# Turning attention probabilities with VectorE blocks and DMA through DRAM, in a one-core two-layer kernel

## The chip, the core and the metric

The kernel runs on one core of a Trainium2 chip. The metric is device time in microseconds of one launch; smaller is better. Before the change the median of three runs is 840.81 us (840.78 to 840.98).

## The reference

The model has two layers on a sequence of 512 tokens of width 1024, everything in float32: first a state-space layer, then a multi-head latent attention layer with 16 heads. The change touches only the second layer. Cut to what it computes there:

```python
def causal_block_attention(q, k, v, scale):          # 16 heads, 512 queries and keys
    s = jnp.einsum('bqhd,bkhd->bhqk', qb, k).astype(jnp.float32) * scale
    s = jnp.where(key_pos[None, :] <= q_pos[:, None], s, -jnp.inf)
    p = jax.nn.softmax(s, axis=-1)
    return jnp.einsum('bhqk,bkhd->bqhd', p, v)

def mla_mixer(u, positions, in_w, q_norm_w, kv_norm_w, uq_w, ukv_w, out_w):
    c_q, c_kv, k_r, z = split(u @ in_w)
    q = rms_norm(c_q, q_norm_w) @ uq_w               # per head 128 + 64 with rotary position
    kv = rms_norm(c_kv, kv_norm_w) @ ukv_w           # per head 128 of k, 128 of v
    o = causal_block_attention(q_full, k_full, v, 192 ** -0.5)
    return (o.reshape(bsz, seq, 2048) * jax.nn.silu(z)) @ out_w

h = h + y                                            # after each layer
return rms_norm(h, final_norm_w)
```

Softmax is taken over the keys of one query, so it is natural to hold scores with the query on the partition. The product with `v` sums over keys, so it wants the key on the partition. The probabilities therefore have to be turned between the two. The residual `h` is turned as well, once: the layers hold it with the feature on the partition, the last step (final norm and output) with the token on the partition.

## The kernel before, in words

**Precision.** A matmul in full precision is done as three matmuls on numbers split into a high part (`hi`, type float32r) and a low part (`lo`, the rest): hi·hi, hi·lo, lo·hi. ScalarE (ACT) makes `hi` with a cast, VectorE (DVE) makes `lo` with a subtraction. This holds for the weights (`split_weight`, tiles `whi`, `wlo`), for activations (`ah`, `al`, `vh`, `vl`, `ch`, `cl`, `qh`, `ql`, `k`) and for the turned probabilities (`ph`, `pl`).

**Weights.** They are streamed: `weight` asks for a tile of a fixed list, and `prefetch` keeps one tile split and one further tile loading ahead. There are two buffers for raw tiles and three for the split ones. All loads are issued by SyncE (SP), which takes its instructions strictly in order and stands still at one whose wait is not met.

**Order of work.** The order on TensorE (PE) is that of the program text. The order on the other engines is made by a scheduler when the program is built; it is fixed then, and each engine takes its instructions in that order. `sched(feed, pieces)` weaves small pieces into a long stream of projections (the feed): a piece is put behind the first projection chunk at which the cost that has gone by reaches the number in a table.

**The attention layer** (`mla`). After six first projections (`U_M1`, loop over `i`) and norms, the heads are worked in pairs: `front_a(j)` projects the rotary part, q and k of the even head, `front_b(j)` q and k of the odd head and v of both, `zgemm` one tile of the gate z. For head `h` the feed is one of the fronts for a later pair, then a `zgemm`, and from head 11 on chunks of the output projection. Into this feed three kinds of pieces are woven, each with its table of shares of the feed's cost:

- `score(h + 1, b)`, table `SC` = 0.0, 0.16, 0.25, 0.44: for the query block `b` of the next head, five matmuls into PSUM (three for block 0), then on DVE the mask and row minimum (L804, L806), on ACT the exponential with its row sum (L223), on DVE the reciprocal (L808) and the scaling (L809). Result: `p`, 128 queries x n keys, n = 128, 256, 384, 512.
- `turn(h, kb)`, table `TU` = 0.02, 0.08, 0.38, 0.55: TensorE transposes (L818) the blocks of key block `kb` of this head, 4, 3, 2 and 1 of 128x128 each, into PSUM tile `pt`; ACT casts them to `ph` (L822), DVE subtracts to `pl` (L823).
- `product(h, kb)`, table `PR` = 0.3, 0.48, 0.65, 0.94: three matmuls (L836) with v; after the last, DVE multiplies with the gate (L838).

In the profile of before, the segment of one head is the stretch from the L797 of `score(h + 1, 0)` to the next L797. "Even" segments are those in which an even head is turned and multiplied; `front_a` runs in them, and so do its four small DMAs `rsw` (L697) that swap 32-partition pieces for the rotary embedding.

**The residual.** In the loop over the six first projections, at i = 2 to 5, TensorE transposes `h` (L682, 32 transposes of 128x128), ACT copies (L685) and SP stores to the DRAM tensor `hd` (L686). It is loaded again much later for the output (L924).

## Time and profile before

| | |
|---|---|
| median of 3 runs | 840.81 us |
| the profiled execution's own time | 840.15 us |
| its span, first to last instruction | 838.3 us |
| granted TensorE clock, mean | 0.998 |
| attention heads, from the first transpose of probabilities to the last | 507.8 to 777.2 us |
| two heads (from one group of `rsw` DMAs at 545.2 to the next at 580.4, 614.9, 650.1) | some 35 us |

The page says for each engine how long it was busy, then shows the span in 40 slices, the DMA queues, and the chain of work that ended last. The trace behind it can be asked for single instructions: start, duration, operation, output and input tiles, and the idle time before with what ended it. A matmul of 512 columns is shown with some 0.39 us, but the next one starts 0.23 us later, since they are pipelined; so the cost of a matmul on TensorE is the distance between starts, not its duration.

### The profile page before, as it was taken

The page shows a single profiled execution, that of the slowest core. Times are in us where ns is not written, and L with a number is a line of the kernel's source. Part 1 is how long each engine was busy: PE and PEld are TensorE (multiplying, and loading weights), DVE is VectorE, ACT ScalarE, POOL GpSimd, SP SyncE. Part 2 cuts the span into 40 slices and gives each one's busy share as a digit, 9 for nine tenths or more (in the row PEclk, how much of TensorE's full clock was granted, in tenths as well). Part 3 has the DMA queues.
Part 4 walks back from the last instruction along what each step waited for, and adds up shares of the span by engine and source line. Part 5 has one row for each costly group of instructions (what it writes and reads, how often), then busy time and mean ns, then how long its engine had stood idle before and what let it go on. Part 6 is the DMA issues. An engine that isn't in the chain of part 4 may idle for free.

```text
span 838.3 us, 11586 instructions
## 1 busy us (share of the span) xinstructions
PE 822.8 (98%) x4260; PEld 694.8 (83%) x4260; DVE 640.2 (76%) x1226; ACT 453.5 (54%) x802; POOL 0.2 (0%) x4
## 2 busy tenths in 40 slices
PE   7999999999999999999999999999999999999996
PEld 5887888888888888888888888888888888888885
DVE  7899898979788979776564887786767869675544
ACT  7567755545565657333354664456547557554233
POOL 0000000000000000000000000000000000000000
PEclk9999999999999999999999999999999999999999
DMA  6354543434242424323225242222221224331212
GB/s 227 102 186 145 153 150 106 147 101 128 98 151 76 151 87 137 121 95 101 90 86 176 79 129 64 77 65 73 73 64 56 89 75 157 100 100 53 92 59 100
DMA packets 35112, 90.55 MB, mean 108 GB/s; under 512 B 4784, under 2 KB 6320, under 8 KB 35056
## 3 DMA queue, kind: packets, MB, share of 16 engines
q1 hardware_dynamic: 34336, 88.77, 32.9%
q10 hardware_dynamic: 720, 1.05, 0.3%
q8 instruction: 33, 0.54, 0.3%
q14 instruction: 23, 0.19, 0.1%
HBM read 83.12 MB, written 4.33 MB: 104 GB/s over the span
## 4 chain that ended last, share of the span: by engine, by line
PE 91%; DVE 5%; DMA 2%; ACT 1%; issue 1%; SPq 0%; DVEq 0%; ACTq 0%
PE mm L291 54%; PE ot L942 11%; PE s L794 5%; PE mm L300 4%; PE po L836 4%; PE mm L774 3%; PE pt L818 2%; PE yd L138 2%; PE yd L291 1%; PE aux L130 1%; PE aux L105 1%; DMA x<-in_x_dram 1%; PE aux L77 1%; PE aux L89 1%; DMA L<-ac_d 1%; DVE wlo L273 1%
## 5 line engine op out<-in xcount | busy, mean ns | idle before, releaser
L272 ACT CAST whi<-raw 128x1024 fp32r<-128x1024 f32 (+3 forms) x132 | 127.0, 965 | 214.7 <-PE mm L291 177.4
L273 DVE TENSOR_TENSOR wlo<-raw,whi 128x1024 fp32r<-128x1024 f32 (+3 forms) x132 | 146.8, 1115 | 56.1 <-ACT whi L272 55.8
L291 PE MATMUL mm<-ah,whi 128*128 128x512 f32 x384 | 153.9, 401 | 0.0
L291 PE MATMUL mm<-ah,wlo 128*128 128x512 f32 x384 | 150.1, 391 | 0.4 <-DVE wlo L273 0.4
L291 PE MATMUL mm<-al,whi 128*128 128x512 f32 x384 | 149.8, 390 | 0.0
L291 PE MATMUL mm<-vh,whi 128*128 128x512 f32 x224 | 89.6, 400 | 0.9 <-ACT whi L272 0.9
L291 PE MATMUL mm<-vh,wlo 128*128 128x512 f32 x224 | 87.8, 392 | 0.7 <-DVE wlo L273 0.7
L291 PE MATMUL mm<-vl,whi 128*128 128x512 f32 x224 | 87.5, 391 | 0.0
L291 PEld LDWEIGHTS mm<-ah,wlo 128*128 128x128 f32 x384 | 72.1, 188 | 16.0 <-DVE wlo L273 0.8
L291 PEld LDWEIGHTS mm<-ah,whi 128*128 128x128 f32 x384 | 72.2, 188 | 15.5 <-issue 1.4
L291 PEld LDWEIGHTS mm<-al,whi 128*128 128x128 f32 x384 | 72.2, 188 | 14.4 <-DVE al L312 0.3
L942 PE MATMUL ot<-whi,ah 128*128 128x512 f32 (+1 forms) x136 | 52.3, 384 | 0.0
L942 PE MATMUL ot<-whi,al 128*128 128x512 f32 (+1 forms) x136 | 51.4, 378 | 0.0
L942 PE MATMUL ot<-wlo,ah 128*128 128x512 f32 (+1 forms) x136 | 51.4, 378 | 0.0
L291 PEld LDWEIGHTS mm<-vh,wlo 128*128 128x128 f32 x224 | 42.0, 188 | 10.8 <-DVE wlo L273 1.5
L291 PEld LDWEIGHTS mm<-vh,whi 128*128 128x128 f32 x224 | 42.1, 188 | 9.2 <-ACT whi L272 1.1
L223 ACT ACTIVATE p<-p,st 128x128 f32<-128x128 f32 (+1 forms) x64 | 36.1, 564 | 25.1 <-DVE st L806 25.0
L291 PEld LDWEIGHTS mm<-vl,whi 128*128 128x128 f32 x224 | 42.2, 188 | 7.2
L822 ACT CAST ph<-pt 128x512 fp32r<-128x512 f32 (+1 forms) x64 | 26.5, 422 | 33.2 <-PE pt L818 32.8
L291 PE MATMUL mm<-ch,whi 128*128 128x512 f32 x104 | 42.6, 409 | 0.0
L291 PE MATMUL mm<-ch,wlo 128*128 128x512 f32 x104 | 40.8, 392 | 0.0
L291 PE MATMUL mm<-cl,whi 128*128 128x512 f32 x104 | 40.7, 392 | 0.0
(225 smaller groups left out, 1642.6 us busy)
## 6 DMA issues: line engine op xcount, KB each, us to landing
raw<-in_w_dram SPq DMA_DIRECT2D x100, 512.0 KB, 3.3
L<-ac_d SPq DMA_DIRECT2D x32, 256.0 KB, 3.8
E<-ea_d SPq DMA_DIRECT2D x32, 128.0 KB, 3.3
raw<-in_ua_dram SPq DMA_DIRECT2D x8, 512.0 KB, 3.3
raw<-in_ub_dram SPq DMA_DIRECT2D x8, 320.0 KB, 2.9
x<-in_x_dram SPq DMA_DIRECT2D x8, 256.0 KB, 4.3
res<-in_x_dram SPq DMA_DIRECT2D x8, 256.0 KB, 3.3
hd<-ht SPq DMA_DIRECT2D x8, 256.0 KB, 2.3
```

What stands on the lines that cost most here:

```text
L138: nc.tensor.matmul(yd[64 * h:64 * h + 64, s], self.xdt[j][:, c, h, :], self.L[2 * j + h][:, s], start=True, stop=True)
L223: i = self.nc.scalar.activation(out, in_, func, **k)
L272: nc.scalar.copy(hi[:, a:b], raw[:, a:b])
L273: nc.vector.tensor_tensor(lo[:, a:b], raw[:, a:b], hi[:, a:b].bitcast(F32), op=ALU.subtract)
L291: self.nc.tensor.matmul(ps, a, b, start=i == 0, stop=i == len(seq) - 1)
L300: self.nc.tensor.matmul(p, seq[i][0], seq[i][1], start=i == 0, stop=i == 3 * ks - 1)
L774: nc.tensor.matmul(ps[:, c2 * 256:(c2 + 1) * 256], a, b, start=i == 0, stop=i == 5)
L794: nc.tensor.matmul(ps[:, :n], x[:, s], y[:, :n], start=k == 0, stop=k == 4)
L818: nc.tensor.transpose(pt[:, (b - kb) * P:(b - kb + 1) * P], probs[h][b][:, kb * P:(kb + 1) * P], self.ident)
L822: nc.scalar.copy(ph[:, :n], pt[:, :n])
L836: nc.tensor.matmul(po[:, kb * P:], x, y, start=kb == 0 and k == 0, stop=kb == NCH - 1 and k == 2)
L942: nc.tensor.matmul(ps[:, a:b], x, y, start=start and i == 0, stop=stop and i == 5)
```

## The change

It takes the transposes of the probabilities and of the residual off TensorE. VectorE's `transpose` turns each 32x32 block of a tile within itself; what is left is to put whole blocks in each other's places. That is done by four DMAs for a tile, one for each band of 32 partitions, that store to a DRAM tensor with runs of 32 numbers (128 bytes). For the probabilities these are two tensors `pd` of 512x512, one for even and one for odd heads; `turn` then loads the turned rows of a key block as `pl`, from which ACT casts `ph` and DVE subtracts in place. There are two buffers `pb` for the turned tiles and one `pl` for each key block. For the residual the same is done with eight tiles of 128x512, stored straight into `hd`.

Two tables change: `SF` puts the scores of head 0 into the feed one projection sooner (`front_b(0)` and `zgemm(4)` are now one feed), and `PR0` puts the products of head 0 later in their feed. The tiles that `norm` uses get other names, so that `pl` is not among them.

```diff
-SF = (0.02, 0.1, 2.1, 3.1)
+SF = (1.0, 1.4, 3.4, 5.0)
+PR0 = (0.5, 0.62, 0.75, 0.95)
...
         hd = self.dram.tile([NCH, P, D], F32, name="hd")
+        turned = hd[:].rearrange("c (j a) d -> a (c j) d", a=32)
...
             if i >= 2:
-                c = i - 2
-                for n in range(2):
-                    pt = self.bank("pt")
-                    for k in range(4):
-                        nc.tensor.transpose(pt[:, k * P:(k + 1) * P], self.h[4 * n + k][:, c * P:(c + 1) * P],
-                                            self.ident)
-                    ht = wk.tile([P, T], F32, tag=("ph", "pl")[n], name=self.nm("ht"))
-                    nc.scalar.copy(ht[:], pt[:])
-                    nc.sync.dma_start(hd[c, :, n * T:(n + 1) * T], ht[:])
+                for k in (2 * i - 4, 2 * i - 3):
+                    ht = wk.tile([P, T], F32, tag="ph", name=self.nm("ht"))
+                    v.transpose(ht[:], self.h[k][:])
+                    for b in range(4):
+                        m = slice(32 * b, 32 * b + 32)
+                        nc.sync.dma_start(turned[:, :, k * P + 32 * b:k * P + 32 * b + 32],
+                                          ht[m, :].rearrange("a (j b) -> a j b", b=32))
...
-        probs = [[] for _ in range(MH)]
+        pd = [self.dram.tile([T, T], F32, name=f"pd{i}") for i in range(2)]
...
             v.tensor_scalar(p[:], p[:], st[:, 2:3], None, op0=ALU.mult)
-            probs[h].append(p)
+            pb = wk.tile([P, T], F32, tag="pb", name=self.nm("pb"))
+            v.transpose(pb[:, :n], p[:])
+            turned = pd[h % 2][:].rearrange("(j a) q -> a j q", a=32)
+            for i in range(4):
+                q = b * P + 32 * i
+                nc.sync.dma_start(turned[:, :n // 32, q:q + 32],
+                                  pb[32 * i:32 * i + 32, :n].rearrange("a (j q) -> a j q", q=32))
...
         def turn(h, kb):
             n = T - kb * P
-            pt = self.bank("pt")
-            for b in range(kb, NCH):
-                nc.tensor.transpose(pt[:, (b - kb) * P:(b - kb + 1) * P], probs[h][b][:, kb * P:(kb + 1) * P],
-                                    self.ident)
+            pl = wk.tile([P, n], F32R, tag=f"pl{kb}", name=self.nm("pl"), bufs=1)
+            nc.sync.dma_start(pl[:].bitcast(F32), pd[h % 2][kb * P:(kb + 1) * P, kb * P:])
             ph = wk.tile([P, T], F32R, tag="ph", name=self.nm("ph"))
-            pl = wk.tile([P, T], F32R, tag="pl", name=self.nm("pl"))
-            nc.scalar.copy(ph[:, :n], pt[:, :n])
-            v.tensor_tensor(pl[:, :n], pt[:, :n], ph[:, :n].bitcast(F32), op=ALU.subtract)
+            nc.scalar.copy(ph[:, :n], pl[:].bitcast(F32))
+            v.tensor_tensor(pl[:], pl[:].bitcast(F32), ph[:, :n].bitcast(F32), op=ALU.subtract)
             parts[h].append((ph, pl))
...
-            at = (wk, ("qh", "ql", "s2") if n == KVL else ("ph", "pl", "s2"))
+            at = (wk, ("qh", "ql", "s2"))
...
-        self.run(front_b(0))
-        self.sched(zgemm(4), [(x, functools.partial(score, 0, b)) for b, x in enumerate(SF)])
+        self.sched(chain(front_b(0), zgemm(4)), [(x, functools.partial(score, 0, b)) for b, x in enumerate(SF)])
...
-            pieces += [(x * cost, functools.partial(product, h, b)) for b, x in enumerate(PR)]
+            pieces += [(x * cost, functools.partial(product, h, b)) for b, x in enumerate(PR0 if h == 0 else PR)]
```

**Where the instructions stand now, SyncE.** The place is the segment of an even head (head 6): its turned probabilities are `pd0`, those of the next, odd head are `pd1`. `raw` are weights, `rsw` the rotary swaps. Before, SP held only these for the two heads:

```order
L263 DMA raw_1149_5729<-in_ub_dram 128x640
L263 DMA raw_1181_5848<-in_uc_dram 128x512
L263 DMA raw_1192_5909<-in_w_dram 128x1024
L697 DMA rsw_1163_5775<-rraw_1162_5773 32x512 x4
L263 DMA raw_1215_5991<-in_ua_dram 128x1024
L263 DMA raw_1231_6057<-in_w_dram 128x1024
```

Now, from the odd head's block 0 on:

```order
L815 DMA pd1_4157<-pb_1152_5847 32x4x32 x4
L823 DMA pl_1153_5853<-pd0_4156 128x512
L823 DMA pl_1155_5858<-pd0_4156 128x384
L697 DMA rsw_1158_5868<-rraw_1157_5866 32x512 x4
L815 DMA pd1_4157<-pb_1165_5901 32x8x32 x4
L815 DMA pd1_4157<-pb_1169_5919 32x12x32 x4
L823 DMA pl_1175_5946<-pd0_4156 128x256
L264 DMA raw_1177_5951<-in_uc_dram 128x512
L815 DMA pd1_4157<-pb_1184_5976 32x16x32 x4
L823 DMA pl_1185_5991<-pd0_4156 128x128
L264 DMA raw_1188_6017<-in_w_dram 128x1024
L823 DMA pl_1196_6047<-pd1_4157 128x512
```

Every load of the even head's probabilities (`pl` from `pd0`) has come to stand behind stores of the next head's scores (`pd1`), which wait for VectorE.

**VectorE, the same segment.** Before, with `p` the scores of the odd head and `pl` those turned of the even head:

```order
L806 ISA p_1154_5746,st_1155_5747<-s_1153_5742,p_1154_5746 128x128
L823 TENSOR_TENSOR pl_1158_5759<-pt_1156_5753,ph_1157_5758 128x512
L808 RECIPROCAL st_1155_5747<-st_1155_5747 128x1
L823 TENSOR_TENSOR pl_1161_5767<-pt_1159_5762,ph_1160_5766 128x384
L809 TENSOR_SCALAR p_1154_5746<-p_1154_5746,st_1155_5747 128x128
L806 ISA p_1168_5802,st_1169_5803<-s_1167_5796,con2_3835 128x256
```

Now (some rows further down on the engine):

```order
L809 TENSOR_SCALAR p_1167_5913<-p_1167_5913,st_1168_5914 128x384
L313 TENSOR_TENSOR ql_1171_5929<-mm_1161_5882,qh_1170_5928 128x512
L723 TENSOR_TENSOR k_1173_5939<-mm_1172_5932,k_1173_5939 128x512
L811 STREAM_TRANSPOSE pb_1165_5901<-p_1163_5895 128x256
L811 STREAM_TRANSPOSE pb_1169_5919<-p_1167_5913 128x384
L826 TENSOR_TENSOR pl_1153_5853<-pl_1153_5853,ph_1154_5855 128x512
L826 TENSOR_TENSOR pl_1155_5858<-pl_1155_5858,ph_1156_5860 128x384
```

The subtraction that makes `pl` of key block 0 stood right behind the row minimum of block 0. It now stands behind the scaling of blocks 1 and 2, the splits of q and k, and two of the new transposes.

Further down in the same segment, now:

```order
L811 STREAM_TRANSPOSE pb_1184_5976<-p_1182_5970 128x512
L826 TENSOR_TENSOR pl_1175_5946<-pl_1175_5946,ph_1176_5948 128x256
L274 TENSOR_TENSOR wlo_1190_6020<-raw_1177_5951,whi_1189_6019 128x512
L712 TENSOR_TENSOR z_1187_6011<-mm_1180_5957,rr_743_3966 128x512
L826 TENSOR_TENSOR pl_1185_5991<-pl_1185_5991,ph_1186_5993 128x128
```

Key block 2's subtraction stands behind the transpose of the odd head's block 3, and key block 3's behind the evacuation `z` of the gate projection; before, both stood ahead of these.

**TensorE, the same segment, now:**

```order
L292 MATMUL mm_1172_5932<-cl_812_4295,whi_1139_5780 128x512
L292 MATMUL mm_1172_5932<-ch_811_4294,wlo_1140_5781 128x512
L839 MATMUL po_1174_5942<-ph_1154_5855,va_1126_5727 128x512
L839 MATMUL po_1174_5942<-ph_1154_5855,vb_1127_5728 128x512
L839 MATMUL po_1174_5942<-pl_1153_5853,va_1126_5727 128x512
```

The order is as it was, less the transposes: `mm_1172` is the projection of k that ACT and DVE split as `k_1173` above, and the products of key block 0 follow it at once.

## The prediction

> **What bounds the kernel now.** I read the page's busy times first, then the chain that ended last, then TensorE's own waits in the attention stage and the busy time of each engine in the two-head stretches.
>
> ```profile
> span 838.3 us, 11586 instructions
> ...
> PE 822.8 (98%) x4260; PEld 694.8 (83%) x4260; DVE 640.2 (76%) x1226; ACT 453.5 (54%) x802; POOL 0.2 (0%) x4
> ...
> PE 91%; DVE 5%; DMA 2%; ACT 1%; issue 1%; SPq 0%; DVEq 0%; ACTq 0%
> ```
>
> ```profile
> PE mm L291 <- DVE wlo L273: 0.2, 1, 0.2
> ```
>
> ```profile
> 545.00:580.00 35.00, 35.00 (x193) 30.45 (x193) 25.18 (x62) 21.80 (x45) 0.00 (x0) 1.00 0.19 57
> 580.00:615.00 35.00, 35.00 (x194) 30.45 (x193) 26.22 (x66) 17.55 (x39) 0.00 (x0) 1.00 0.27 84
> ```
>
> The columns of the last fence are window, length, busy us of PE, PEld, DVE, ACT and POOL, granted clock, DMA share and GB/s. TensorE is busy throughout, and the middle fence is the whole list of its waits from 480 to 790 us: one, of 0.2 us. So in the attention stage each us taken off TensorE is a us gained, and each wait put on it is a us lost, since its order is fixed and nothing can slip past a waiting matmul. VectorE works 75% of that stretch, DMA 19 to 27%.
>
> **What the change removes.** The transposes:
>
> ```profile
> L818 PE MATMUL pt<-ident,p x160: 270/272/276, 507.9 to 777.4; 128*128 128x128 f32 x160
> ```
> ```profile
> L682 PE MATMUL pt<-ident,res x32: 270/272/273, 442.9 to 462.6; 128*128 128x128 f32 x32
> ```
>
> ```profile
> 577.16 0.28 PE L797 MATMUL s<-k,qh 128*128 128x256 f32 x1
> ...
> 577.33 0.34 PE L799 MATMUL s<-k,s 128*128 128x256 f32 x1
> 577.51 0.93 PE L818 MATMUL pt<-ident,p 128*128 128x128 f32 x7
> 578.19 0.48 PE L291 MATMUL mm<-ch,whi 128*128 128x512 f32 x1
> 578.50 0.39 PE L291 MATMUL mm<-cl,whi 128*128 128x512 f32 x1
> ```
>
> Seven transposes hold the start of the next matmul back by 0.68 us, and that one's successor comes after 0.31 instead of 0.23 us: 0.76 us for 7, 0.11 us each. 192 of them are **21.1 us** (3.5 of it the residual's). Taken alone the profiled 840.15 us would become 819.
>
> **What it puts on TensorE: waits.** I follow one even head in the trace of before, shift TensorE's starts by the transposes gone, and ask when the new route delivers. These are the matmuls that need it:
>
> ```profile
> 583.89 0.39 PE L836 MATMUL po<-ph,va 128*128 128x512 f32 x1
> ...
> 584.35 0.40 PE L836 MATMUL po<-pl,va 128*128 128x512 f32 x1
> ...
> 586.89 0.62 PE L794 MATMUL s<-k,s 128*128 128x512 f32 x2
> ...
> 589.28 0.36 PE L836 MATMUL po<-ph,va 128*128 128x256 f32 x1
> ...
> 589.60 0.28 PE L836 MATMUL po<-pl,va 128*128 128x256 f32 x1
> ...
> 592.47 0.22 PE L836 MATMUL po<-ph,va 128*128 128x128 f32 x1
> ...
> 600.28 0.40 PE L836 MATMUL po<-ph,va 128*128 128x512 f32 x1
> ```
>
> Key block 0 was due at 583.89, now at 583.1 (7 transposes less), its third matmul at 583.6. Two chains lead to it. Their prices:
>
> ```profile
> 578.79 0.28 DVE L804 TENSOR_TENSOR p<-s,con 128x128 f32<-128x128 f32 x1
> 579.11 0.29 DVE L806 CUSTOM_DVE_ANT_0 p<-s,p 128x128 f32<-128x128 f32 x1
> ...
> 579.97 0.16 DVE L808 RECIPROCAL st<-st 128x1 f32<-128x1 f32 x1
> ...
> 580.51 0.28 DVE L809 TENSOR_SCALAR p<-p,st 128x128 f32<-128x128 f32 x1
> ```
> ```profile
> L223 ACT ACTIVATE p<-p,st 128x512 f32<-128x512 f32 x16 | 11.6, 724 | 5.1 <-DVE st L806 5.0
> L823 DVE TENSOR_TENSOR pl<-pt,ph 128x512 fp32r<-128x512 f32 x16 | 11.0, 690 | 3.7 <-ACT ph L822 3.7
> L806 DVE CUSTOM_DVE_ANT_0 p<-s,con 128x512 f32<-128x512 f32 x16 | 10.9, 681 | 0.2 <-PE s L794 0.2
> ...
> L822 ACT CAST ph<-pt 128x512 fp32r<-128x512 f32 x16 | 9.4, 588 | 26.0 <-PE pt L818 26.0
> ...
> L806 DVE CUSTOM_DVE_ANT_0 p<-s,con 128x384 f32<-128x384 f32 x16 | 8.8, 550 | 3.1 <-PE s L794 3.1
> ...
> L809 DVE TENSOR_SCALAR p<-p,st 128x512 f32<-128x512 f32 x16 | 7.7, 481 | 0.2
> ...
> L806 DVE CUSTOM_DVE_ANT_0 p<-s,con 128x256 f32<-128x256 f32 x16 | 6.8, 423 | 6.1 <-PE s L794 6.1
> ...
> L822 ACT CAST ph<-pt 128x256 fp32r<-128x256 f32 x16 | 5.9, 370 | 0.4
> ```
> ```profile
> L697 SPq DMA_DIRECT2D rsw<-rraw x32: 507/586/792, 483.0 to 719.9; - x32
> ```
> ```profile
> L686 SPq DMA_DIRECT2D hd<-ht x8: 319/324/601, 444.8 to 464.1; - x8
> L924 SPq DMA_DIRECT2D hr<-hd x8: 319/320/332, 695.3 to 707.9; - x8
> ```
> ```profile
> hd<-ht SPq DMA_DIRECT2D x8, 256.0 KB, 2.3
> ...
> hr<-hd SPq DMA_DIRECT2D x8, 256.0 KB, 2.9
> ```
>
> *The DMA chain.* SP takes the four stores of the odd head's block 0 before the even head's first load. The scaled block 0 ends at 580.8; less some 0.3 us, since two subtractions that stood between are gone from there: 580.5. The 32x32 transpose has no row; L806 and L809, VectorE operations of the same size, take 0.29 and 0.28: 580.8. A store issued from 32 partitions has its nearest row in `rsw`, 0.59 us each (bounds: 0.32, the plain 128-row store, and 1.28, if issue grew with the runs of 128 bytes, 512 instead of 128): 4 x 0.59, 583.1. The load lands 2.9 us later as `hr` does, 586.0; cast 0.59, 586.6. TensorE waits 3.5 us; the subtraction (0.69, 587.3) adds 0.3. **3.8 us.**
>
> *The VectorE chain, if DMA cost nothing.* The k projection ends where key block 0 begins; its cast and split (0.58 and 0.68, as `qh` and `pl` of that size), the transposes of blocks 1 and 2 (0.42 and 0.55, as L806) and the subtraction stand ahead of the third matmul: 583.1 + 0.2 + 0.58 + 0.68 + 0.97 + 0.69 = 586.2 against 583.6, **2.6 us**. The DMA chain is longer and decides.
>
> *Key block 1* is loaded right behind block 0, and is in time.
>
> *Key block 2.* On SP the first two loads (0.32 each), four `rsw` and eight stores go ahead: 583.1 + 0.64 + 12 x 0.59 = 590.8; landing 2.9, cast 0.37, subtraction about 0.42 (as L806 of that size): 594.1 and 594.5. It was due at 589.28 - 0.99 (nine transposes) + 3.8 = 592.1. **2.2 us.** By VectorE alone: from the end of the scores of block 3 (587.5 in the trace) to the third matmul at 589.60 are 2.0 us, one transpose less; row minimum 0.68, exponential 0.72, reciprocal 0.16, scaling 0.48, transpose 0.68 (as L806) and subtraction 0.42 make 3.1: 1.3 us.
>
> *Key block 3* stands on VectorE behind the gate's evacuation, which waits for the last matmul before this product:
>
> ```profile
> 592.67 0.69 DVE L712 TENSOR_TENSOR z<-mm,rr 128x512 f32<-128x512 f32 x1 [1.90 <-PE mm L291]
> ```
>
> 0.2 + 0.69 + 0.28 against 0.2 to the third matmul: **1.0 us**, whatever DMA does.
>
> *Odd heads.* Their first load comes after block 3's stores have landed, near 595.6 on this clock, so data is there at 599.8; the product, at 600.28 - 1.9 + 7.0 = 605.4, doesn't wait.
>
> So an even head waits 3.8 + 2.2 + 1.0 = 7.0 us; eight of them 56 us. Heads 14 and 15 have a thinner feed, and a weight load that waits for ACT stands ahead of the last stores; I bound that by 0 and 10 us and take 5. The bounds for the four unseen prices: with VectorE alone (2.6 + 1.3 + 1.0) x 8 = 39; with 0.8 us a store (the slowest `rsw`) 4 and 8 stores add 0.84 and 1.7, so 76; with 1.28 us, 5.5 a head more on key block 2 and 2.8 on block 0, 122.
>
> **What is hidden.** 72 transposes on VectorE add at most 0.68 us each, 3.9 us for two heads beside 25 to 26 busy of 35. The weights that now queue behind the probabilities on SP: `w` is issued near 594.2 and landed by 597.5, split by 599.8, and used only after the odd head's product 0, at 605. If that cover went, the gate projection would be late next. The residual's 32 stores (19 us of SP) lie beside six projections, and `hd` is read 230 us later. Head 0's tables give it more room than other heads; I count it like them.
>
> **Packets.** Two heads store 2 x 5120 runs of 128 bytes, 640 for each of 16 DMA engines.
>
> ```profile
> q10 hardware_dynamic: 144, 0.00, 1.3%
> ```
> ```profile
> q10 hardware_dynamic: 720, 1.05, 0.3%
> ```
>
> The first row is that queue in the first 6 us: 144 packets of 32 bytes or less in 1.3% of 16 x 6 us, 8.7 ns each. The second is its whole span, some 56 ns for a mean of 1.46 KB. In between, 128 bytes lie near 13 ns: 8 us per two heads on engines now 19 to 27% busy. The upper bound, 56 ns, would be 36 us per two heads.
>
> The Trainium skill, "DMA: Bandwidth & Descriptors", section Specifications, holds that under 512 bytes a transfer is below line rate and is read, modified and written. By it a run would cost like 512 bytes twice, which between the two rows is 2 x 25 ns, an estimate, and would lead to the third rival; no row of before has such a store, and the 8.7 ns packets speak against it for reads.
>
> **The sum.** 840.15 - 21.1 + 56 + 5 = 880.1 in the profiled execution's own time; the median of the runs is 0.7 us above that one: **881 us**.
>
> **Rivals.**
> 1. *VectorE's order alone* (DMA is faster than its nearest rows): 840.8 - 21.1 + 39 = 859. For it: 3.8 against 2.6 is a small difference made of five DMA prices. Against it: each of them has a row.
> 2. *Faster: the route fits into TensorE's other work.* The gain is 21.1 us over eight even heads, 2.6 each; the change pays only if an even head waits less. That needs the split of k to be done before product 0 and the new transposes to take next to nothing; at 1.0 us a head (key block 3 alone) it would be 840.8 - 21.1 + 8 = 828. Against it: the k projection ends exactly where product 0 starts.
> 3. *SP or the DMA engines become the bound.* Two heads need 32 stores, 8 loads, 4 `rsw` and 5 weight loads: 36 x 0.59 + 13 x 0.32 (for every plain load) = 25.4 of some 40 us, but at 1.28 us a store 47. By the sums above 840.8 - 21.1 + 76 + 5 = 901 at 0.8 us and 947 at 1.28; with 56 ns a packet DMA needs 36 + 8 = 44 us per two heads, 4 more than the 40 now forecast, 913.
> 4. *The clock drops.* The two-head rows above show it granted at 1.00, with TensorE never idle. The Trainium skill, "TensorE: Matmul & The Clock Gate", Part 1, says that an idle window of about 3.4 us halves the clock until it has been busy as long. My longest wait, 3.5 us, is just there; eight times 1.7 us lost would make 895, an estimate by that page. The trace of before has no such wait in it, so it can't show this, and I give it no chance of its own.
>
> **How the numbers follow.** My forecast has 0.63 (866 to 900), VectorE alone 0.13 (near 859), SP or DMA as the bound 0.18 (900 to 950), the faster one 0.05, no change 0.01. The range from 856 to 930 leaves out the faster cases and the dearer half of the third rival. A difference of 0.2%, 1.7 us, is about what can be told from no change: faster 0.05, same 0.01, slower 0.94.
>
> **What would show it.** Right: TensorE's list of waits has the product's line (now L839) on ACT `ph` and DVE `pl`, near 7 us per two heads and in even segments alone; SP waits on VectorE's `pb`; stores take some 0.6 us to issue. Rival 1: those waits name VectorE mostly and sum to 39. Rival 3: SP is issuing without a pause, weights come late, and L292 waits too. Wrong: no waits at L839, and two heads in under 33 us.

## The result, and the profile after

The changed kernel takes **899.33 us** (median of 4 runs, 897.67 to 901.59) against 840.89 us before (840.78 to 841.21), a ratio of 1.070, 95% interval 1.067 to 1.072: 58.4 us slower. The forecast was 881 us, slower, with 856 to 930 as the range. So the sign and the mechanism of the waits came out, and the size was 18 us short.

The page of the changed kernel, its busy times, its clock in 40 slices, and the chain that ended last:

```profile
span 897.5 us, 11852 instructions
PE 830.3 (93%) x4068; PEld 686.5 (76%) x4068; DVE 675.8 (75%) x1298; ACT 453.0 (50%) x794; POOL 0.2 (0%) x4
...
PEclk9999999999999999999999999999999979898999
...
PE 76%; DVE 8%; DMA 7%; SPq 3%; ACT 2%; issue 2%; DVEq 0%; ACTq 0%
```

TensorE was 98% busy and is now 93%. DMA and SP's queue, which were 2% of the chain together, are 10% of it. And the clock, which was full all the way, has dips in the second half. TensorE's waits from 480 to 850 us, the whole list (what waited, for what, us in total, times, longest):

```profile
PE po L839 <- ACT ph L825: 41.3, 19, 5.1
PE po L839 <- DVE pl L826: 10.2, 12, 2.1
PE s L797 <- DVE k L723: 0.8, 1, 0.8
PE mm L292 <- DVE wlo L274: 0.5, 1, 0.5
```

Where there was one wait of 0.2 us there are 31 at the product, 51.5 us in all, each of them in an even head's segment. ACT, which casts `ph`, waits in its turn for the load, 39.4 of 50.1 us:

```profile
L825 ACT CAST ph<-pl 128x512 fp32r<-128x512 f32 (+1 forms) x64 | 28.0, 457 | 50.1 <-DMA pl<-pd 39.4
```

And SP, which issues the load, waits most for VectorE's `pb`, 40.6 us in the same stretch. These are the signs that the prediction named for itself. By key block (the first matmul, which needs `ph`, and the third, which needs `pl`; the number behind the bar is busy time, then the idle time ahead of it):

```profile
L839 PE MATMUL po<-pl,va 128*128 128x512 f32 x16 | 8.3, 521 | 0.8 <-DVE pl L826 0.8
L839 PE MATMUL po<-ph,va 128*128 128x512 f32 x16 | 7.8, 485 | 23.5 <-ACT ph L825 23.5
...
L839 PE MATMUL po<-pl,va 128*128 128x256 f32 x16 | 5.4, 336 | 6.9 <-DVE pl L826 6.9
...
L839 PE MATMUL po<-ph,va 128*128 128x256 f32 x16 | 5.2, 325 | 6.0 <-ACT ph L825 5.9
L839 PE MATMUL po<-pl,va 128*128 128x128 f32 x16 | 5.0, 311 | 2.5 <-DVE pl L826 2.5
...
L839 PE MATMUL po<-ph,va 128*128 128x128 f32 x16 | 4.3, 267 | 11.9 <-ACT ph L825 11.9
```

Key block 0 costs 24.3 us, key block 2 12.9, key block 3 14.4, key block 1 nothing: over eight even heads 3.0, 1.6 and 1.8 us each, 6.4 together (7.0 was forecast). One of these segments, first single rows of VectorE, ACT and TensorE, then SP's queue:

```profile
592.35 0.31 DVE L811 STREAM_TRANSPOSE pb<-p 128x128 f32<-128x128 f32 x1
...
597.67 1.04 ACT L825 CAST ph<-pl 128x512 fp32r<-128x512 f32 x2 [1.33 <-DMA pl<-pd]
...
598.34 0.50 PE L839 MATMUL po<-ph,va 128*128 128x512 f32 x1 [2.62 <-ACT ph L825]
```
```profile
594.82 0.81 SPq L823 DMA_DIRECT2D pl<-pd  x2
...
598.20 5.03 SPq L815 DMA_DIRECT2D pd<-pb  x8
603.33 0.41 SPq L823 DMA_DIRECT2D pl<-pd  x1
...
605.74 1.94 SPq L815 DMA_DIRECT2D pd<-pb  x4
607.79 0.44 SPq L823 DMA_DIRECT2D pl<-pd  x1
```

The odd head's block 0 is transposed by 592.7, its four stores follow, and only then the even head's load is issued, at 594.8. Its data is cast at 597.7, and TensorE, which could have begun at 595.7, begins at 598.3. The loads of key blocks 2 and 3 (603.3 and 607.8) stand behind the odd head's next stores in the same way.

**The clock.** The waits are not the whole loss. Here is the same segment cut where the clock's own steps lie, every 3.41 us (columns as in the windows above: PE is the third number, the granted clock stands behind the five engines):

```profile
597.33:600.75 3.41, 2.40 (x9) 1.72 (x10) 2.83 (x6) 1.04 (x2) 0.00 (x0) 1.00 0.52 122
600.75:604.16 3.41, 3.25 (x15) 2.40 (x14) 2.84 (x6) 2.06 (x4) 0.00 (x0) 1.00 0.41 68
604.16:607.57 3.41, 1.34 (x6) 1.09 (x7) 2.20 (x6) 1.02 (x2) 0.00 (x0) 1.00 0.67 153
607.57:610.99 3.41, 3.41 (x9) 2.63 (x8) 0.37 (x1) 0.30 (x1) 0.00 (x0) 0.50 0.64 158
```

A window in which TensorE is busy 1.34 of 3.41 us is followed by one at half the clock: 9 matmuls in it, against 15 in a window at full clock. The mean granted clock of the profiled run fell from 0.998 to 0.975, which over 897.5 us is 0.023 x 897.5 = 20.6 us of full clock.

**The sum.** -21.1 (transposes, as forecast) + 51.5 + 20.6 = +51.0, of a measured +58.4. Some 7 us are not itemised. An estimate for most of them: a matmul of 512 columns is shown with 0.39 us but costs 0.23 in a full pipeline, so an idle time that is counted from its end leaves out 0.16 us of what the wait costs, 5 us for 31 waits.

### The profile page after: what moved, and what is told of

The parts are those of the page before. It is cut to its first block, busy times and chain, and to the rows that moved or that the text cites. A ratio compares the mean times of both kernels' runs of the same rounds, so it can differ in the third digit from the quotient of the medians.

```text
span 897.5 us, 11852 instructions
## 1 busy us (share of the span) xinstructions
PE 830.3 (93%) x4068; PEld 686.5 (76%) x4068; DVE 675.8 (75%) x1298; ACT 453.0 (50%) x794; POOL 0.2 (0%) x4
## 4 chain that ended last, share of the span: by engine, by line
PE 76%; DVE 8%; DMA 7%; SPq 3%; ACT 2%; issue 2%; DVEq 0%; ACTq 0%
PE mm L292 46%; PE ot L944 9%; DMA pl<-pd 4%; PE mm L301 4%; PE s L794 3%; PE po L839 3%; PE mm L774 3%; SPq L815 2%; PE yd L139 2%; PE yd L292 1%; PE aux L131 1%; PE aux L106 1%; DMA x<-in_x_dram 1%; DVE wlo L274 1%; PE aux L78 1%
## 5 line engine op out<-in xcount | busy, mean ns | idle before, releaser
L292 PE MATMUL mm<-vh,whi 128*128 128x512 f32 x224 | 91.7, 410 | 0.3 <-ACT whi L273 0.2
L292 PE MATMUL mm<-vh,wlo 128*128 128x512 f32 x224 | 90.4, 404 | 1.0 <-DVE wlo L274 1.0
L292 PE MATMUL mm<-vl,whi 128*128 128x512 f32 x224 | 90.6, 404 | 0.0
L292 PEld LDWEIGHTS mm<-al,whi 128*128 128x128 f32 x384 | 72.2, 188 | 14.4 <-DVE al L313 0.3
L839 PE MATMUL po<-ph,va 128*128 128x512 f32 (+1 forms) x64 | 22.6, 353 | 41.4 <-ACT ph L825 41.3
L825 ACT CAST ph<-pl 128x512 fp32r<-128x512 f32 (+1 forms) x64 | 28.0, 457 | 50.1 <-DMA pl<-pd 39.4
L292 PEld LDWEIGHTS mm<-vh,wlo 128*128 128x128 f32 x224 | 44.0, 196 | 11.9 <-DVE wlo L274 1.9
L839 PEld LDWEIGHTS po<-ph,va 128*128 128x128 f32 x64 | 12.2, 191 | 52.4 <-ACT ph L825 51.0
L292 PEld LDWEIGHTS mm<-vl,whi 128*128 128x128 f32 x224 | 44.1, 197 | 8.6
```

The source lines that it names most:

```text
L292: self.nc.tensor.matmul(ps, a, b, start=i == 0, stop=i == len(seq) - 1)
L825: nc.scalar.copy(ph[:, :n], pl[:].bitcast(F32))
L839: nc.tensor.matmul(po[:, kb * P:], x, y, start=kb == 0 and k == 0, stop=kb == NCH - 1 and k == 2)
```

## The experiments

After the result my theory was: the loads come late because they stand on SP's queue behind stores that wait for VectorE; those waits cost 51 us, and the halved clock behind them another 20. The rivals were VectorE's own order (the first rival of the prediction), the packets, and that the halved clock lies in time that is waited anyway. The table gives all runs; "waits" are those at the product from 480 to 850 us, "clock" is the mean granted one.

| run | us | ratio to before, 95% | waits, us | clock |
|---|---|---|---|---|
| changed kernel | 899.3 | 1.067 to 1.072 | 51.5 | 0.975 |
| e1 residual only | 836.4 | 0.994 to 0.996 | 0 | 0.997 |
| e2 probabilities only | 906.0 | 1.075 to 1.080 | 47.5 | 0.975 |
| e3 waits filled | 888.1 | 1.054 to 1.059 | 26.7 | 0.989 |
| e4 one store a block | 832.0 | 0.989 to 0.992 | 7.5 | 0.995 |
| e5 four stores, long runs | 869.8 | 1.034 to 1.037 | 28.2 | 0.981 |
| e6 even heads only | 851.5 | 1.011 to 1.014 | 13.7 | 0.990 |
| e7 odd heads only | 869.3 | 1.033 to 1.037 | 25.1 | 0.981 |
| e8 products later | 898.0 | 1.066 to 1.070 | 49.2 | 0.971 |
| e9 load first | 893.0 | 1.059 to 1.067 | 45.6 | 0.972 |
| e10 e5, store first | 875.8 | 1.038 to 1.044 | 33.1 | 0.979 |
| e11 eight stores a block | 977.2 | 1.158 to 1.167 | 114.5 (480 to 905) | 0.934 |
| e12 reordered | 875.0 | 1.037 to 1.042 | 32.2 | 0.980 |

e4, e5 and e10 leave out the right order of the probabilities, so only their times count. And the engines' order is made anew for every kernel: on SP's queue e2, e3 and e8 have the changed kernel's order but for a weight load or two, and in e9 little has moved beside the load of key block 0, while in e4, e5, e10 and e11 more has moved, on one engine or another, than the edit says.

### The two parts by themselves: e1 and e2

e1 is the kernel before with the residual's hunk of the diff alone; e2 is the changed kernel with that hunk taken back.

> The residual's turn alone; the probabilities stay with TensorE's transposes. My theory: 32 transposes at 0.11 us leave TensorE's path, 3.5 us, and nothing waits in their place, since the copy is read 230 us later: 840.9 - 3.5 = 837.4 us, ratio 0.996. Rival: the residual's 32 stores take SP's queue from the weights of the same projections, so a projection waits and the gain is gone: 841 us or more, with a wait at L292 between 440 and 480 us.

> The probabilities' turn alone; the residual is turned by TensorE as before. If the two parts do not touch each other, this is the changed kernel plus the residual's 3.5 us: 899.3 + 3.5 = 902.8 us, the waits at the product 50 to 56 us and the granted clock 0.97 to 0.98. Rival: the residual's part costs something in the changed kernel (its stores, its later reads), so this comes out at 899 or below.

e1 measured 836.39 us (835.92 to 837.01), 4.3 us faster than before where 3.5 was forecast. Its TensorE waits are those of before, so the 32 stores and the copy that is read 230 us later are hidden. e2 measured 905.95 us (901.84 to 908.57): the whole loss is the probabilities', and the residual's part gains 6.6 us in the changed kernel too (it was 3.5 by the sum; the spread of e2's runs is as wide as the difference). The waits at the product are 47.5 us, a little under the 50 to 56 expected. The rival of each falls.

### Is the halved clock a cost of its own? e3

```diff
             po = acc[h]
+            if h % 2 == 0:
+                for _ in range((7, 0, 4, 3)[kb]):
+                    nc.tensor.matmul(self.fill[:], self.onesr[:], k12[:, 0], start=True, stop=True)
```

> The changed kernel with 14 matmuls of no use put into TensorE's queue in each even head, 7 ahead of the product of key block 0, 4 ahead of key block 2, 3 ahead of key block 3: 112 matmuls of 512 columns, 0.23 us each, 25.8 us more work, all into a bank that nobody reads. An even head waits 6.4 us on average, more than the 3.2 us of its fillers, so they should lie in the waits. My theory now, that some 20 us of the loss are the halved clock behind each wait: the waits named at the product fall by some 20 to 26 us, the granted clock stays at 0.99 or above, and the kernel becomes faster by the clock's part: 880 us, 877 to 888. Rival, that the halved clock lies in time that is waited anyway and costs nothing: 899 us. Rival, that a filler holds the next stage back as any matmul does: 905 to 925 us.

The matmuls write to a PSUM bank of their own, so the other tiles have 7 banks instead of 8. The waits of e3, and its windows where the changed kernel had (PE busy, clock) 30.47 at 0.90 and 34.34 at 0.96:

```profile
PE po L843 <- ACT ph L826: 21.9, 20, 3.7
PE po L843 <- DVE pl L827: 4.8, 8, 1.4
```
```profile
545.00:580.00 35.00, 32.87 (x166) 27.04 (x165) 26.18 (x65) 16.98 (x37) 0.00 (x0) 1.00 0.49 128
580.00:620.00 40.00, 37.87 (x189) 31.18 (x188) 29.76 (x72) 22.63 (x46) 0.00 (x0) 1.00 0.52 132
```

112 matmuls that nobody reads, 25.8 us of work, made the kernel **11.2 us faster**. They took the place of 24.8 us of waits, and the clock stayed up: 0.989 against 0.975 is 12.4 us. So the halved clock is a cost of its own, and a filler in a wait costs next to nothing. The time missed the expected 880 (and just missed the 877 to 888), because the clock still fell in the last two even heads, where waits of up to 3.7 us stayed beside the fillers.

### SP's queue or VectorE's order? e4

```diff
-            turned = pd[h % 2][:].rearrange("(j a) q -> a j q", a=32)
-            for i in range(4):
-                q = b * P + 32 * i
-                nc.sync.dma_start(turned[:, :n // 32, q:q + 32],
-                                  pb[32 * i:32 * i + 32, :n].rearrange("a (j q) -> a j q", q=32))
+            turned = pd[h % 2][:].rearrange("(j a) q -> a j q", a=P)
+            nc.sync.dma_start(turned[:, :b + 1, b * P:(b + 1) * P], pb[:, :n].rearrange("a (j q) -> a j q", q=P))
```

> One store for a block of the turned probabilities instead of four: 128 partitions, runs of 128 queries (512 bytes) instead of 32, so SP issues 4 stores a head and not 16 and a quarter of the packets move. The four 32-row bands of a block land in the wrong order, so the order of the probabilities is left out of what is computed; every wait and every other instruction is there. The chain that I predicted runs through SP's queue: 3 x 0.45 us less ahead of key block 0 and 6 x 0.45 less ahead of key block 2, of waits of 2.3 to 2.6 and 1.3 to 2.2; what stays is about 1 us at key block 0 and 1 us at key block 3, 2 us an even head: 840.9 - 21.1 + 16 = 836 us, 832 to 845, with the clock at 0.99 or above. Rival 1 of the prediction, VectorE's order: its waits stay whatever SP does, 39 us by the prediction: 859 us, or 875 with the clock halved behind them.

It took 831.96 us, 8.7 us faster than before. TensorE's waits at the product and SP's rows of the stores (count, then shortest, median and longest issue in ns):

```profile
PE po L836 <- ACT ph L822: 7.2, 4, 2.2
...
PE po L836 <- DVE pl L823: 0.3, 1, 0.3
```
```profile
L813 SPq DMA_DIRECT2D pd<-pb x64: 319/371/822, 495.2 to 755.9; - x64
```

The 64 transposes and 64 subtractions on VectorE are all there, and of the waits 7.5 us are left, nearly all in four odd heads. So VectorE's work did not have to cost 39 us: that rival falls as a floor. But e4 doesn't part SP's queue from the order of the other engines, since all of it has changed: in seven of the eight even heads all four loads stand on SP ahead of the odd head's first store (in the changed kernel none does), and on ACT and VectorE the cast and the subtraction for key block 0 stand ahead of those of k. What speaks against the rival in the changed kernel itself is that ACT waited for the DMA. VectorE's order has its part all the same: DVE `pl` is named for 10.2 us, and SP's stores wait for `pb`. e4 also says what the route would be worth if a block could be stored in one piece and the orders came out as here. I found no single store that also puts the 32x32 blocks in their right places.

### The number of issues or the packets? e5, e10 and e11

e5 keeps four stores of 32 partitions, with runs of 512 bytes as in e4 (a quarter of the packets). e10 is e5 with the even head's load of key block 0 put back behind the odd head's stores of block 0. e11 goes the other way: each store of the changed kernel cut in two, with the same packets.

```diff
 e5, with e4's `turned`:
+                m = slice(32 * i, 32 * i + 32)
+                nc.sync.dma_start(turned[m, :b + 1, b * P:(b + 1) * P], pb[m, :n].rearrange("a (j q) -> a j q", q=P))
 e10, beside that:
+            st = stores.get((h + 1, 0)) if kb == 0 and h % 2 == 0 else None
+            with tc.issue_after(st.ins) if st else ExitStack():
+                nc.sync.dma_start(pl[:].bitcast(F32), pd[h % 2][kb * P:(kb + 1) * P, kb * P:])
 e11:
-            for i in range(4):
+            for i in range(8):
+                q, a = b * P + 32 * (i // 2), 16 * (i % 2)
+                nc.sync.dma_start(turned[a:a + 16, :n // 32, q:q + 32],
+                                  pb[16 * i:16 * i + 16, :n].rearrange("a (j q) -> a j q", q=32))
```

> Four stores a block as in the changed kernel, each from 32 partitions, but with runs of 128 queries (512 bytes) instead of 32, a quarter of the packets. The runs land in the wrong order, so the order of the probabilities is left out of what is computed, as with the single store. Theory A, the number of issues on SP's queue is the price: the issue stays near 0.45 us, waits at the product 45 to 55 us, 890 to 900 us. Theory B, the packets are the price (DMA engines busy, or an issue that grows with the runs it describes): the issue falls towards 0.3 us or the landing gets shorter, and the time comes close to the single store's 832: 832 to 855 us.

> The changed kernel with each store cut in two, of 16 partitions each: twice the issues on SP's queue, with the same packets and bytes and everything computed. Theory A, an issue costs some 0.45 us whatever it describes: four more issues ahead of key block 0 (1.8 us) and eight more ahead of key block 2 (3.6 us) in each even head, 43 us in all, 942 us, and since SP then needs 64 x 0.45 + 13 x 0.4 + 4 x 0.5 = 36 us of a pair's 41, odd heads begin to wait too and the clock loses more: 942 to 1000 us. Theory B, an issue's cost goes with the runs it describes: half a store costs half, and the time stays: 895 to 905 us.

> The kernel with four stores a block of 512-byte runs, which took 869.8 us, with the order on SP's queue put back to that of the changed kernel in one place: an even head's load of key block 0 behind the odd head's four stores of block 0. As there, the runs land in the wrong order. Theory A, the order on SP's queue was what that kernel gained by: key block 0 waits 2 us in each even head again, 16 us and 3 to 7 us of clock: 885 to 895 us. Theory B, the longer runs were what it gained by, through shorter issues and transfers: 868 to 874 us.

The stores on SP in the changed kernel, e5 and e11, a fence each:

```profile
L815 SPq DMA_DIRECT2D pd<-pb x256: 302/449/1686, 494.5 to 821.6; - x128
```
```profile
L815 SPq DMA_DIRECT2D pd<-pb x256: 302/425/1552, 495.0 to 794.6; - x128
```
```profile
L815 SPq DMA_DIRECT2D pd<-pb x512: 302/432/1615, 495.0 to 893.6; - x171
```

The median issue takes 0.43 to 0.45 us whether it describes 512 runs of 128 bytes at most, a quarter as many, or half as many. Within the changed kernel it rises a little, from 0.43 us for the 128 runs of block 0 to 0.49 for the 512 of block 3. So twice the issues is nearly twice the time on SP, and theory B falls. e11 lies in theory A's range, 977.2 us with the clock at 0.934, but by luck in part: the waits are 114.5 us where 51 + 43 was worked out, all in even heads where odd ones were to wait too, and the most of what was added is at key block 0:

```profile
L839 PE MATMUL po<-ph,va 128*128 128x512 f32 x16 | 9.5, 595 | 73.2 <-ACT ph L825 73.2
...
L839 PE MATMUL po<-ph,va 128*128 128x256 f32 x16 | 6.0, 374 | 26.9 <-ACT ph L825 26.9
```

Key block 0 waits 73.2 us, 6.1 more in each even head than in the changed kernel. Its four further issues are 1.8 of them. VectorE's order has changed as well: the odd head's block 0 is scaled, and then turned only behind the scores of blocks 1 and 2 and the splits of q and k:

```profile
612.26 0.29 DVE L809 TENSOR_SCALAR p<-p,st 128x128 f32<-128x128 f32 x1
...
615.89 0.63 DVE L811 STREAM_TRANSPOSE pb<-p 128x128 f32<-128x128 f32 x2
```

From the end of the scaling to the transpose are 2.5 to 8.1 us in e11's odd heads, 0 to 0.8 in the changed kernel's. SP has nothing else ahead of these stores and stands idle until the transpose is done, 4.1 us in this segment. So e11 shows that the price of an issue hardly goes with what it describes; the 78 us that it lost are not the price of 256 issues alone.

e5 did not come out as either theory: 869.8 us, with the issue price hardly changed. Its key block 0 hardly waits (5.5 us in all, 24.3 in the changed kernel), and SP's rows show a reason:

```profile
582.14 0.35 SPq L264 DMA_DIRECT2D raw<-in_w_dram  x1
582.73 0.34 SPq L822 DMA_DIRECT2D pl<-pd  x1
584.07 1.72 SPq L815 DMA_DIRECT2D pd<-pb  x4
```

The scheduler that sets the order when the program is built put this load ahead of the odd head's stores, and the gate's weight ahead of both; it is so in six of eight even heads, and in five the cast of `ph` also stands ahead of that of k on ACT. The wait moves to key block 2, 22.2 us against 12.9, whose load stands behind eight stores as before (in seven heads):

```profile
L838 PE MATMUL po<-ph,va 128*128 128x256 f32 x16 | 5.4, 338 | 18.3 <-ACT ph L824 18.3
```

With that one place put back, in e10, key block 0 waits 20.6 us again and the time rises by 6 us, to 875.8: the order there is real, but it is a fifth of what e5 gained. Of the other 24 us between e10 and the changed kernel the trace shows where most of the waits went: e10 waits 18.4 us less, 13.8 of it at key block 3 (0.6 us against 14.4). Its load is the second of these two, and the stores are those of the odd head's block 3:

```profile
594.38 1.80 SPq L825 DMA_DIRECT2D pl<-pd  x2
...
600.87 1.76 SPq L816 DMA_DIRECT2D pd<-pb  x4
```

The load stands ahead of these stores in seven of eight even heads, in the changed kernel behind them in all eight. So in e10, too, it is a place on SP's queue that goes with the gain. Whether longer runs have a part in it stays **open**: no run changes them alone.

### Which heads? e6 and e7

In both, the heads that are left out go by TensorE's transposes as before.

```diff
+            if not (h % 2 == 0):        # e7: h % 2 == 1
+                probs[h].append(p)
+                return
             pb = wk.tile([P, T], F32, tag="pb", name=self.nm("pb"))
```

> Only the even heads' probabilities go by VectorE and DMA, the odd heads' by TensorE as before; the residual as in the changed kernel. 80 transposes at 0.11 us leave TensorE, 8.8 us, so without any wait 836.4 - 8.8 = 827.6. My prediction's chain puts the odd head's four stores of block 0 on SP ahead of the even head's first load, and eight more ahead of its third; they are gone here. Theory A, that chain is the cause: key blocks 0 and 2 don't wait, key block 3 waits 1.0 behind the gate's evacuation: 827.6 + 8 = 836, 828 to 845, clock above 0.99. Theory B, the even head waits for its own chain (its own 16 stores, landing, the order of VectorE), whatever the odd head does: 6.4 us a head stay, and the halved clock with them: 827.6 + 51 + 10 to 20 = 889 to 899 us.

> Only the odd heads' probabilities go by VectorE and DMA, the even heads' by TensorE as before; the residual as in the changed kernel. My prediction said that odd heads don't wait, and none did in the changed kernel. Theory A, they have slack of their own: 836.4 - 8.8 = 827.6 us, up to 832, no waits at the product. Theory B, their slack came from the even heads' waits just before, 6.4 us in which their stores and loads went ahead; without these they wait themselves, 2 to 5 us each: 827.6 + 16 to 40, and some halved clock, 845 to 880 us.

e6 took 851.5 us: without the odd head's stores ahead of the load, key blocks 2 and 3 don't wait, and key block 0 waits 13.7 us in eight heads instead of 24.3. What is left in a typical segment, 1.2 us, has its row on ACT:

```profile
584.30 0.58 ACT L722 CAST k<-mm 128x512 fp32r<-128x512 f32 x1 [0.30 <-PE mm L292]
584.80 1.15 ACT L840 CAST ph<-pl 128x512 fp32r<-128x512 f32 x2
```

The cast of `ph` stands behind that of k, which can't start before k's projection ends, and the product comes right after that projection. This is the chain that the first rival spoke of, on ACT and worth 1.2 us, not 2.6. e6 lies between its two theories, nearer to A.

e7 took 869.3 us and refutes a step of mine. Odd heads were said not to wait, and in the changed kernel none does. Alone they wait 24.3 us at key block 0:

```profile
L854 PE MATMUL po<-pl,va 128*128 128x512 f32 x16 | 8.8, 549 | 3.5 <-DVE pl L841 3.4
L854 PE MATMUL po<-ph,va 128*128 128x512 f32 x16 | 7.4, 465 | 20.9 <-ACT ph L840 20.9
```

Their slack in the changed kernel was made by the even head's waits just before. The way from a head's last scores to its turned key block 0 is longer than TensorE's work in between, for either kind of head. e4 agrees: there even heads don't wait at key block 0, and four odd ones do, 7.2 us.

### More time, another order: e8, e9 and e12

e8 gives every head the later products that the change gives to head 0. e9 turns one place on SP's queue round: the even head's load of key block 0 ahead of the odd head's stores of block 0. e12 orders everything anew.

```diff
 e8:
-enumerate(PR0 if h == 0 else PR)
+enumerate(PR0)
 e9:
+            ld = loads.get((h - 1, b)) if b == 0 and h % 2 == 1 else None
+            with tc.issue_after(ld.ins) if ld else ExitStack():
                 for i in range(4):
...
+            at = ((0.03,) + SC[1:] if h % 2 == 0 else SC) if h + 1 < MH else ()
 e12, with e9's rule for block 0 of all heads and without PR0; first tuple of a table for even segments:
+SC = ((0.0, 0.19, 0.2, 0.23), (0.06, 0.24, 0.25, 0.57))
+TU = (-0.04, -0.03, 0.0, 0.2)
+PR = ((0.34, 0.48, 0.69, 0.73), (0.3, 0.56, 0.87, 0.87))
```

> The changed kernel with all heads' products where it has only head 0's: at 0.5, 0.62, 0.75 and 0.95 of a head's feed instead of 0.3, 0.48, 0.65 and 0.94. Of an even head's feed of 17 us that is 3.4 us more for key block 0, 2.4 for key block 1, 1.7 for key block 2, 0.2 for key block 3. Theory A, the chains are as long as I worked them out and end at a fixed distance from the scores: the waits of 2.3 to 2.6 and 1.3 to 2.2 us at key blocks 0 and 2 are gone, those at key block 3 stay: 836.4 - 17.6 + 8 to 15 = 827 to 834 us. Theory B, later products also hold the buffers of the loads and the casts longer, so the loads behind them on SP's queue start later and the next products wait instead: 880 to 905 us.

> The changed kernel, with one thing turned round on SP's queue: an even head's load of key block 0 is issued ahead of the odd head's four stores of block 0, which have to wait for VectorE, and not behind them. To make room, the scores of that block 0 come 3% of a feed (0.5 us) later in TensorE's order. Everything is computed, and the number of issues is the same. Theory A, the order on SP's queue is what makes key block 0 late: its waits, 23 us of the 51 in the changed kernel, shrink to the 1.2 us a head that ACT's and VectorE's order left in the kernel with even heads alone, 10 us, and some of the halved windows go with them: 875 to 888 us. Theory B, what gives way there comes back at key blocks 1 to 3, since SP still has 16 stores a head to issue: 892 to 900 us.

> Everything computed and every issue kept, 16 stores a head, but the order mended as a whole: loads are asked for ahead of the next head's scores, a block 0's stores always behind the load of key block 0 before it, loads of key block 2 ahead of the blocks 1 and 2, the last scores of even heads earlier, and the products of an odd head later. Theory A, the order makes up for most of what the waits cost: key block 3 does not wait, key block 0 keeps the 1.2 to 2 us that ACT's and VectorE's order leaves, key block 2 about 1 us, 2.5 to 3.5 us an even head (20 to 28 in all), waits short enough that the clock loses 5 to 10 us only: 840.7 - 21.1 + 24 + 8 + 7 (what the sums of the runs so far leave over) = 859, 852 to 872. Theory B, as with the load first: what is won at one key block is lost at the next: 885 to 900 us. In neither does it come below the 836.4 of the residual alone.

e8: 898.0 us, no gain. Key block 0 waits 15.1 us instead of 24.3, but key block 3 waits 22.5 instead of 14.4. My reason for theory B, buffers held longer, isn't what the rows show; the load of key block 3 stands, as before, behind four stores that start when VectorE lets them:

```profile
607.66 1.94 SPq L815 DMA_DIRECT2D pd<-pb  x4
609.70 0.44 SPq L823 DMA_DIRECT2D pl<-pd  x1
```

e9: 893.0 us, close to theory B. A typical even head waits 1.2 to 1.4 us for `ph` at key block 0, as in e6, where it waited 2.3 to 2.6. So the place behind the odd head's stores is about half of that wait, and the rest is the cast behind that of k. The whole of key block 0 falls only from 24.3 to 20.3 us, since 0.2 to 0.4 us for `pl` come on top and heads 0, 12, 14 and 15 wait longer. Key block 2 now takes 15.6 us in all (12.9 in the changed kernel), and the clock is no better (0.972):

```profile
L842 PE MATMUL po<-pl,va 128*128 128x256 f32 x16 | 5.7, 358 | 6.7 <-DVE pl L829 6.7
...
L842 PE MATMUL po<-ph,va 128*128 128x256 f32 x16 | 5.2, 325 | 8.9 <-ACT ph L828 8.9
```

e12: 875.0 us, 24 us better than the changed kernel with all its 256 stores, 3 us over the range of theory A. Waits are down to 32.2 us and spread over even and odd heads. It is still 34 us slower than before. So the order, that of the products included, holds some 24 us of the loss, and none of the orders I ran makes up for 16 stores a head.

**The version that beats both kernels** is e1, the residual alone: 836.4 us, 0.5% faster than before.

## Why the prediction came out as it did

**What bounds it, and the transposes.** Right. TensorE's order lets nothing slip past a waiting matmul, and each wait became time. The 32 transposes of the residual were worth 4.3 us, not 3.5.

**The chain to key block 0.** Every link is in the trace, with sizes off in both directions; but e6 and e9 show that without its first link, the odd head's stores, 1.2 of some 2.4 us stay, for the cast of `ph` behind that of k on ACT, which the prediction had as a shorter chain beside it. Store issue: 0.59 forecast, 0.45 measured. Load: 2.9 from issue to landing forecast, 3.6 measured as the median of `pl` of that size, 2.9 in the segment shown. Wait: 3.8 forecast, 3.0 measured. The 32x32 transpose was priced by L806 at 0.29 to 0.68 us and takes 0.31 to 0.71:

```profile
L811 DVE STREAM_TRANSPOSE pb<-p 128x512 f32<-128x512 f32 x16 | 11.3, 709 | 0.5
...
L811 DVE STREAM_TRANSPOSE pb<-p 128x128 f32<-128x128 f32 x16 | 4.9, 307 | 0.3
```

**Key block 2**: 2.2 forecast, 1.6 measured. **Key block 3**: 1.0 forecast, 1.8 measured, and the cause was wrong. "Whatever DMA does", the prediction said, with VectorE behind the gate's evacuation; but 11.9 of its 14.4 us wait for ACT's `ph`, and ACT for the load:

```profile
L825 ACT CAST ph<-pl 128x128 fp32r<-128x128 f32 x16 | 4.8, 298 | 29.9 <-DMA pl<-pd 24.2 <-PE po L839 5.5 <-ACT whi L273 0.2
```

In e6, where the odd head's stores are gone, key block 3 does not wait at all; in e10, where its load stands ahead of the last four of them, it waits 0.6 us.

**Odd heads don't wait.** True of the changed kernel and false as a reason: e7. The waits were counted in the right heads because the even head, first in the queue, pays for both.

**The sum of waits** was 61 with heads 14 and 15, and 51.5 were measured.

**What failed** is the fourth rival: "eight times 1.7 us lost would make 895", and "I give it no chance of its own". The waits were forecast 10 us too long, yet the time 18 us too short, because the clock took 20.6 us that the sum had no term for (-10 + 21, and the 7 not itemised). That 899.3 still lies within the 866 to 900 of the forecast is luck in part: waits that were forecast too long made up for half of the term left out. I had compared single waits with a whole window and found only the longest, 3.5 us, long enough. The Trainium skill ("TensorE: Matmul & The Clock Gate", Part 1: The HAM clock gate) names an idle window of about 3.4 us as the condition; the window's length agrees with the traces (the changed kernel's half-clock stretches between 480 and 850 us are 3.41 us long, one is twice that), the condition does not: much less than a whole idle window is enough, as told below. The twelve halved windows of the profiled run, at 1.7 us each, would have made the forecast 881 + 20 = 901.

**Packets.** The price of near 13 ns fits. The loads' and stores' queue in e1 (packets, MB, share of 16 engines):

```profile
q1 hardware_dynamic: 50080, 88.77, 34.1%
```

Before, it was 34,336 packets and 32.9%. For the residual, 16,384 packets of 128 bytes take the place of 1,024 of 2 KB, and the queue's time rises from 0.329 x 16 x 838.3 us to 0.341 x 16 x 834.0, by 137 us: 8.4 ns for each short one if the long ones had cost nothing, 13 ns if they had cost some 80 ns each (an estimate, the 56 ns for 1.46 KB taken to 2 KB). In the changed kernel the queue has 43.0% of 897.5 us; over e1 that is at most 20 ns for each of the 81,920 short packets of the probabilities, if all else there cost nothing. The 50 ns that I had worked out by the Trainium skill's rule on short transfers ("DMA: Bandwidth & Descriptors", Specifications) do not show here.

**SP as the bound**, the third rival, is not what the changed kernel does, but it is the direction in which its cost lies: at twice the issues (e11) it is 977 us, further up than that rival's 947, a part of it by VectorE's order.

## What to carry to other kernels

When work is moved from a saturated engine to a DMA route, count the issues on the queue and ask what each load stands behind: a load behind a store that waits for another engine is as late as that engine, and shifting the consumer or one load alone mostly moves the wait to the next load (e8, e9, e5). When a variant is built by a scheduler, read its order before giving the difference to the edit. When a wait is put on TensorE, add a second term for the clock; a wait of 2 us can cost nearly as much again, and matmuls of no use in the wait take that term away. And take a change apart: the part that paid here, the residual, had 230 us of slack and was hidden in the loss of the other.

## What the runs showed of the hardware that I had not expected

**The clock reacts to less than an idle window.** I split the stretch from 480 to 815 us of the changed kernel and of e2 to e12 at the clock's own 3.41 us steps and took the share of each window without a matmul, for windows at full clock. After 63 windows that were idle for 62% or more, the next was at half clock 63 times; after 968 idle for less than 50%, 9 times, all of them idle for 46% or more; between 50 and 62%, 14 times of 19. The least idle window that was followed by half clock had 46%, the most idle one that was not had 56%. So some 1.6 to 1.9 us of idle time within one window decide, in one wait or in several, and it depends on how a wait lies to the steps: the wait of 2.6 us at 595.7 to 598.3 fell into two windows and cost nothing more, the one of 2.2 us at 604 to 606 halved the next window.

**An issue on SP costs nearly the same whatever it describes**: in the median 0.43 us for a store of 128 runs of 128 bytes and 0.49 for one of 512 (32 partitions, changed kernel), 0.42 to 0.46 for 16 partitions (e11), 0.42 to 0.43 for runs of 512 bytes (e5), 0.37 us for a store of 128 partitions (e4).
